# An expert's steps in a new traced order, with three engines' orders pinned to it

## The chip, the cores and the metric

One core of one Trainium2 chip runs the whole program. The metric is device time in microseconds (us); for the kernel before it is 1950.55 us, the median of three runs (1948.15 to 1952.71). The engines are named as in the profile: PE is TensorE (PEld its weight loads), DVE is VectorE, ACT is ScalarE, POOL is GpSimd, SP issues the DMAs.

## What is computed

Two encoder layers on 256 tokens of width 1024, in f32. Each layer has a token mixer, a cross-attention, and a channel mixer, each followed by a residual sum and a layer norm. The channel mixer of the second layer is a mixture of eight experts, of which each token uses two. The change touches that part alone:

```python
D_MODEL, SEQ, N_EXPERTS, TOP_K, D_FF_EXPERT = 1024, 256, 8, 2, 3584

def moe_swiglu(x, w_router, w_gate, w_up, w_down):
    logits = x @ w_router                               # (256, 8)
    top_logit, top_e = lax.top_k(logits, TOP_K)
    top_w = jax.nn.softmax(top_logit, axis=-1)
    # for each expert e and the tokens xs that chose it:
    #   hdn = jax.nn.silu(xs @ w_gate[e]) * (xs @ w_up[e])
    #   y[tokens] += top_w * (hdn @ w_down[e])
```

The weights of one expert are three matrices of 1024 x 3584 f32, 44 MB; all eight are read, whatever the routing gives.

## The kernel before

**Tiling.** `moe` (line 1285) routes the tokens and then calls `expert_run(range(NE), slot, late=True)`. For each expert `gather` collects up to 128 of its tokens with selection matmuls and transposes (`ps_gr`, `ps_gt`) into `xg`, as a high part, a low part and, as `gw`, whole f32. The hidden width 3584 is cut into `NC` = 7 chunks of 512 columns. A chunk has six weight pieces of 1 MiB each: two of `moe_wg` (g0, g1), two of `moe_wu` (u0, u1) and two of `moe_wd` (d0, d1). The products of a chunk are the gate g, the up product u (each 8 contraction slices into one PSUM bank `ps_gu`) and the down product d, which adds four slices into the two banks `ps_ye` and is done one chunk later than g and u.

**Pieces.** `wload` (line 302) issues a piece's DMA into a raw buffer `wr` (SP, line 309) and splits it into `wh`, a copy in fp32r on ScalarE (line 325, two instructions of 128x1024), and `wl = wr - wh` on VectorE (line 331, two instructions). There are nine raw buffers in this part and four pairs of `wh`, `wl`, both used in rotation, so a piece takes over the split pair of the piece four places before it and the raw buffer of the piece nine places before it.

**Two forms of a product.** `products` (line 1389) holds both under a condition on the expert's count of tokens. Over 64 tokens, `passes` makes three matmuls for each slice (`h wh`, `h wl`, `l wh`; lines 1394 to 1396) from the split pieces. Up to 64, `paired` makes one f32 matmul for each slice straight from the raw piece (line 1402), in two halves of the array that `fold` adds up (line 1419, from a copy `fe`, line 1418). The splits stand under the same condition on ScalarE and VectorE and are skipped for an expert with up to 64 tokens. The first form is called dense below and the second sparse.

**Between g, u and d.** `hidden` (line 1440) makes `hs = silu(g) * u`: a Silu on ScalarE (line 1442) and a product on VectorE (line 1443). There is one `hs` buffer. `down` (line 1446) transposes `hs` on TensorE (four instructions into `ps_hT`, line 1449), copies it on ScalarE as `hw` (line 1453) and `hh` (line 423), subtracts for `hl` on VectorE (line 423) and then runs the products with d0 and d1. After an expert's last chunk `combine` scales `ye` and adds it to `x` (lines 1475 to 1501).

**Order.** The program is traced, and a planner then puts each engine's instructions into a fixed queue order by priorities and its own estimate of times. The traced order of a chunk n is: load and split g0, g1; g; copy `fe`; load and split u0, u1; u; copy `fe`; transposes of chunk n-1; `hw`, `hh`, `hl`; load and split d0; product; load and split d1; product; Silu and `hs` of chunk n. The planner is free to deviate, but for one chain: `in_turn` (line 295) pins the split copies of ScalarE, and these alone, in the order in which they are traced. It does this with dependencies that cost no semaphore. What stands under a condition is planned as one block.

Of the kernel before, what the change touches and what calls it, by code (L numbers as in the profile page):

```python
# [10 lines left out]
F32 = mybir.dt.float32  # L11
# [8 lines left out]
P = 128  # L20
# [143 lines left out]
def tile_encoder(ctx: ExitStack, tc: tile.TileContext, a: dict, out: bass.AP, cw: dict):  # L164
# [125 lines left out]

    where = _offsets()

    split = []
# [991 lines left out]
    def moe(l, i, xh, xl, xth, xtl):  # L1285
        with weights("r3", NX, ring=raws), tc.tile_pool(name="mo", bufs=1, reuse_waits="tile") as O:
# [97 lines left out]
            def expert_run(experts, sl, late=False):  # L1384

                NC = FE // 512
                pend = []

                def products(many, ws, h, l, hw, fold=None):


                    def passes():
                        for out, k, wh, wl, _, b, z in ws:
                            T.matmul(out, h[:, k], wh, start=b, stop=False)  # L1394
                            T.matmul(out, h[:, k], wl, start=False, stop=False)  # L1395
                            T.matmul(out, l[:, k], wh, start=False, stop=z)  # L1396

# [23 lines left out]
                parted = lambda many: () if many is None else many[1:]  # L1421

                def gate_up(e, gs, many, c, late=False):
                    pgu, fo = [], None
                    for ws in ("moe_wg", "moe_wu"):
                        pt = abank("ps_gu")
                        todo = []
                        for kh in range(2):
                            wh, wl, w = wload(ws, i * NE + e, kh * 4, 4, c * 512, 512,
                                              [ln_end[0], pd_end[0]] if late else (), parted(many))  # L1430
                            for k4 in range(4):
                                k = kh * 4 + k4
                                todo.append((pt, k, wh[:, k4], wl[:, k4], w[:, k4], k == 0, k == KT - 1))
                        products(many, todo, *gs, fo)
                        pgu.append(pt)
                        if many is not None:
                            fo = folds(e, pt)
                    return pgu, fo

                def hidden(pgu):  # L1440
                    hs = O.tile([P, 512], F32, name="hs", tag="hs", bufs=HSB)
                    A.activation(hs, pgu[0], AF.Silu)
                    V.tensor_mul(hs, hs, pgu[1])  # L1443
                    return hs

                def down(e, many, c, hs, ye, fo):
# [10 lines left out]
                    for f0 in (0, 2):  # L1457

                        ahead = ends if e == experts[-1] and c == NC - 1 and f0 else ()
                        dh, dl, w = wload("moe_wd", i * NE + e, 4 * c + f0, 2, 0, D, ahead, parted(many))  # L1460
                        todo = []
                        for n in range(2):
                            for f in range(2):
                                b, z = c == 0 and f0 + f == 0, c == NC - 1 and f0 + f == 3
                                ns = slice(n * 512, n * 512 + 512)
                                todo.append((ye[n], f0 + f, dh[:, f, ns], dl[:, f, ns], w[:, f, ns], b, z))
                        products(many, todo, hh, hl, hw, fo if f0 else None)

                def combine(e, many, ye, first):

# [29 lines left out]
                            else:  # L1500
                                V.tensor_add(xs, xs, po)

                def flush(fo=None):
                    e, many, c, hs, ye = pend.pop()
                    if c == 0:
                        ye[:] = [bank(psb, "pb", "ps_ye") for _ in range(2)]
                    down(e, many, c, hs, ye, fo)
                    if c == NC - 1:
                        combine(e, many, ye, late and e == experts[0])

                fold = {}
# [6 lines left out]
                for n, e in enumerate(experts):  # L1518
                    gs, many = nxt
                    if many is not None:  # L1520
                        folding(e)
                    ye = []
                    for c in range(NC):
                        pgu, fo = gate_up(e, gs, many, c, late and n + c == 0)
                        if pend:
                            flush(fo if c else None)
                        if fo and not c:
                            fo()
                        hs = hidden(pgu)
                        pend.append((e, many, c, hs, ye))  # L1530
                        if c == NC - 3 and n + 1 < len(experts):
                            nxt = gather(experts[n + 1], sl)
                flush()

            expert_run(range(NE), slot, late=True)
            lp = act.tile([P, 2, D], F32, name="lp", tag="opTh")
# [107 lines left out]
```

## Time and profile before

| what | us |
|---|---|
| median of three runs | 1950.55 |
| the profiled execution: its own time | 1953.46 |
| the profiled execution: span from first to last instruction | 1951.7 |
| first expert's stretch in that span (dense) | 942 to 1104 |
| five sparse experts | 1104 to 1629 |
| two dense experts and the end | 1629 to 1952 |

The page of the profile gives busy time by engine (PE 1733.4 us, DVE 1070.0, ACT 902.8), the span in forty slices with TensorE's granted clock, and the DMA rate in each slice. Busy PE is modelled and grows when the clock is halved, so what tells of lost time in a stretch is the start of one product to the start of the next, and the idle time that stands in brackets in a timeline. In a timeline a row is a run of like instructions: start, length, engine, line, operation, tiles written and read, count, and in brackets the idle time of the engine before it and what ended it.

### The profile page before, as it was taken

What the parts mean: (1) busy time and instruction counts of PE and PEld (TensorE: products, weight loads), DVE (VectorE), ACT (ScalarE), POOL (GpSimd) and SP (SyncE); (2) the same over time, 40 slices, a digit from 0 to 9 for tenths busy, and PEclk for the clock granted to TensorE, in tenths of its full rate; (3) what the DMA queues carried; (4) which work ended last, traced back from release to release, by engine and by line L of the source; (5) the groups of instructions that cost most, each with busy time, mean ns of one, the idle gap of its engine ahead of it and who ended that gap; (6) DMA issues with size and microseconds to landing.
All of it is one profiled execution on the core that took longest, in us unless ns stands there. A gap on an engine that the chain in (4) does not pass through costs nothing. (4 is left out here: it accounts for less than half of the span.)

```text
span 1951.7 us, 29900 instructions
## 1 busy us (share of the span) xinstructions
PE 1733.4 (89%) x11084; PEld 1216.1 (62%) x11084; DVE 1070.0 (55%) x1755; ACT 902.8 (46%) x1651; POOL 257.5 (13%) x248
## 2 busy tenths in 40 slices
PE   6888999999978898998678999899999998999995
PEld 5767779899967776696456633333333334776773
DVE  6887666755568966674565612111111114776785
ACT  4754435555536554452565522122212223776673
POOL 4545310000046453011000000000000000000000
PEclk8988999999989888998788999999999998999997
DMA  6321255455423312551366899999999999878790
GB/s 218 110 102 67 88 194 196 174 177 188 143 81 118 104 67 88 207 224 65 132 256 259 308 405 420 420 419 420 419 420 420 420 420 384 309 282 306 289 359 34
DMA packets 71301, 473.93 MB, mean 243 GB/s; under 512 B 8768, under 2 KB 12224, under 8 KB 15936
## 3 DMA queue, kind: packets, MB, share of 16 engines
q1 hardware_dynamic: 70384, 466.09, 61.7%
q10 hardware_dynamic: 720, 5.24, 0.7%
q8 instruction: 119, 1.95, 0.4%
q14 instruction: 78, 0.64, 0.1%
HBM read 470.26 MB, written 1.05 MB: 241 GB/s over the span
## 5 line engine op out<-in xcount | busy, mean ns | idle before, releaser
L331 DVE TENSOR_TENSOR wl<-wr,wh 128x1024 fp32r<-128x1024 f32 (+4 forms) x530 | 482.5, 965 | 132.9 <-ACT wh L325 131.5
L325 ACT ACTIVATE wh<-wr 128x1024 fp32r<-128x1024 f32 (+1 forms) x564 | 436.0, 845 | 104.4 <-issue 27.9
L1402 PE MATMUL ps_gu<-wr,gw 128*64 128x512 f32 x1120 | 273.7, 615 | 24.6 <-DMA wr<-in_moe_wg_dram 22.6
L1402 PEld LDWEIGHTS ps_gu<-wr,gw 128*64 128x64 f32 x1120 | 81.0, 140 | 178.4 <-issue 141.3
L1453 ACT ACTIVATE hw<-ps_hT 128x512 f32<-128x512 f32 x56 | 33.4, 596 | 334.1 <-PE ps_hT L1449 333.9
L1394 PE MATMUL ps_gu<-wh,xg 128*128 128x512 f32 x336 | 142.6, 424 | 13.6 <-ACT wh L325 13.2
L1402 PE MATMUL ps_ye<-wr,hw 128*64 128x512 f32 x560 | 151.1, 598 | 3.3 <-DMA wr<-in_moe_wd_dram 3.2
L1395 PE MATMUL ps_gu<-wl,xg 128*128 128x512 f32 x336 | 141.2, 420 | 10.3 <-DVE wl L331 10.3
L334 POOL TENSOR_TENSOR wl<-wr,wh 128x384 fp32r<-128x384 f32 (+6 forms) x68 | 103.9, 1549 | 290.3 <-ACT wh L325 289.9
L423 DVE TENSOR_TENSOR hl<-ps_hT,hh 128x512 fp32r<-128x512 f32 x56 | 38.7, 690 | 186.3 <-ACTq L317 107.7
L1396 PE MATMUL ps_gu<-wh,xg 128*128 128x512 f32 x336 | 138.9, 413 | 0.0
L1568 POOL TENSOR_TENSOR x<-x,lp 128x512 f32<-128x512 f32 x1 | 1.8, 1800 | 1021.5 <-ACT x L1567 1021.5
L1443 DVE TENSOR_TENSOR hs<-hs,ps_gu 128x512 f32<-128x512 f32 x56 | 38.3, 685 | 177.8 <-PE ps_gu L1419 173.0
L1418 ACT ACTIVATE fe<-ps_gu 128x512 f32<-128x512 f32 x112 | 66.8, 597 | 102.5 <-PE ps_gu L1419 93.0
L1272 PE MATMUL ps_gu<-xTl,wh 128*128 128x256 f32 x352 | 99.2, 282 | 0.0
L1273 PE MATMUL ps_gu<-xTh,wl 128*128 128x256 f32 x352 | 99.1, 282 | 0.0
L1271 PE MATMUL ps_gu<-xTh,wh 128*128 128x256 f32 x352 | 99.0, 282 | 0.0
L1402 PEld LDWEIGHTS ps_ye<-wr,hw 128*64 128x64 f32 x560 | 49.3, 136 | 79.3 <-issue 56.1
L1394 PEld LDWEIGHTS ps_gu<-wh,xg 128*128 128x128 f32 x336 | 68.3, 203 | 33.2 <-ACT wh L325 16.4
L1395 PEld LDWEIGHTS ps_gu<-wl,xg 128*128 128x128 f32 x336 | 68.4, 203 | 31.4 <-DVE wl L331 17.1
L1419 PE MATMUL ps_gu<-fe,fold 128*64 128x512 f32 x146 | 76.4, 605 | 8.0 <-ACT fe L1418 8.0
L1396 PEld LDWEIGHTS ps_gu<-wh,xg 128*128 128x128 f32 x336 | 67.9, 202 | 15.3
(469 smaller groups left out, 3723.1 us busy)
## 6 DMA issues: line engine op xcount, KB each, us to landing
wr<-in_moe_wg_dram SPq DMA_DIRECT2D x112, 1024.0 KB, 15.8
wr<-in_moe_wu_dram SPq DMA_DIRECT2D x112, 1024.0 KB, 16.3
wr<-in_moe_wd_dram SPq DMA_DIRECT2D x112, 1024.0 KB, 16.1
wr<-in_w_in_dram SPq DMA_DIRECT2D x16, 1024.0 KB, 4.8
wr<-in_ffn_wg_dram SPq DMA_DIRECT2D x11, 1024.0 KB, 4.9
wr<-in_ffn_wu_dram SPq DMA_DIRECT2D x11, 1024.0 KB, 4.9
wr<-in_ffn_wd_dram SPq DMA_DIRECT2D x11, 1024.0 KB, 4.9
wr<-in_xk_dram SPq DMA_DIRECT2D x8, 1024.0 KB, 4.9
```

What stands on the lines that cost most here:

```text
L325: act_i = A.activation(h[:, s], raw[:, s], AF.Copy)
L331: V.tensor_sub(l[:, m], raw[:, m], R_(h[:, m]))
L334: G.tensor_sub(l[:, m], raw[:, m], R_(h[:, m]))
L1271: T.matmul(ps[:, g], wh[:, k, fs], xh[:, k, :], start=k == 0, stop=False)
L1272: T.matmul(ps[:, g], wh[:, k, fs], xl[:, k, :], start=False, stop=False)
L1273: T.matmul(ps[:, g], wl[:, k, fs], xh[:, k, :], start=False, stop=k == KT - 1)
L1394: T.matmul(out, h[:, k], wh, start=b, stop=False)
L1395: T.matmul(out, h[:, k], wl, start=False, stop=False)
L1396: T.matmul(out, l[:, k], wh, start=False, stop=z)
L1402: T.matmul(out[f * HALF:f * HALF + HALF], hw[:, k, :HALF], w, start=ws[j][5], stop=ws[j + 1][6], skip_group_check=True)
L1418: A.activation(fe, pt, AF.Copy)
L1419: return lambda: T.matmul(pt[:HALF], fold[e], fe, start=False, stop=True, skip_group_check=True)
```

## The change

Only `expert_run`, `wload` and `in_turn` change. `in_turn` keeps one chain per engine. Into ScalarE's chain go the split copies, the `fe` copies, `hw`, `hh` and the Silu; into VectorE's the split subtractions, `hl` and the product `hs`; into TensorE's the first matmul of each dense product and the transposes. The last piece's wait for the last `hh` and `hl` (`ahead`) is taken out.

The splits are no longer traced where their product is traced. `order` lists the pieces in the order of before, and `split(n)` loads and splits the next n of them. For a chunk n the traced order becomes: g; split d0 of chunk n-1; transposes of n-1 with `hw`, `hh`, `hl`; split d1 of n-1; `fe` of g; u; split g0 of n+1; `fe` of u; d of n-1 (and `combine` after an expert's last); Silu of n; split g1 and u0 of n+1; product `hs` of n; split u1 of n+1; and `gather` of the next expert after the fifth chunk. The number of instructions of each kind, the DMAs and the buffers stay the same.

```diff
     def in_turn(i):
-        if split:
-            tc.add_manual_dep(i.ins, split[-1].ins.name, mybir.DependencyInfo(
+        e = i.ins.engine
+        if e in pinned:
+            tc.add_manual_dep(i.ins, pinned[e].ins.name, mybir.DependencyInfo(
                 mybir.DependencyClass.NoSync, mybir.DependencyReason.DATA), reason="in_turn")
-        split[:] = [i]
+        pinned[e] = i
...
-                    V.tensor_sub(l[:, m], raw[:, m], R_(h[:, m]))
+                    dve_i = V.tensor_sub(l[:, m], raw[:, m], R_(h[:, m]))
+                    if whole:
+                        in_turn(dve_i)
...
+                turn = lambda many, *ins: [in_turn(i) for i in ins if many is not None]
...
-                        for out, k, wh, wl, _, b, z in ws:
-                            T.matmul(out, h[:, k], wh, start=b, stop=False)
+                        for j, (out, k, wh, wl, _, b, z) in enumerate(ws):
+                            i = T.matmul(out, h[:, k], wh, start=b, stop=False)
+                            if j == 0:
+                                turn(many, i)
...
-                    A.activation(fe, pt, AF.Copy)
+                    in_turn(A.activation(fe, pt, AF.Copy))
...
-                    for f in range(4):
-                        T.transpose(pT[:, f], hs[:, f * P:f * P + P], ident)
+                    turn(many, *[T.transpose(pT[:, f], hs[:, f * P:f * P + P], ident) for f in range(4)])
...
-                        A.activation(hw, pT, AF.Copy)
+                        turn(many, A.activation(hw, pT, AF.Copy))
...
-                    ends = evac_split(hh, hl, pT)
...
+                    turn(many, *evac_split(hh, hl, pT))
...
+                steps = [(e, c) for e in experts for c in range(NC)]
+                order, made = [], {}
+                for n, step in enumerate(steps):
+                    order += [(*step, "g", 0), (*step, "g", 1), (*step, "u", 0), (*step, "u", 1)]
+                    if n:
+                        order += [(*steps[n - 1], "d", 0), (*steps[n - 1], "d", 1)]
+                order += [(*steps[-1], "d", 0), (*steps[-1], "d", 1)]
...
+                def downs(many, e, c, hs, ye, fo):
+                    split()
+                    parts = turned(many, hs)
+                    split()
+                    yield
...
+                    for j in range(2):
+                        down(many, c, 2 * j, parts, ye, made.pop((e, c, "d", j)), fo() if j else None)
+                    if c == NC - 1:
+                        combine(e, many, ye, late and e == experts[0])
+                    yield
...
+                split(4)
+                prev = None
+                for n, (e, c) in enumerate(steps):
...
+                    gates(gs, ptg, ws[0], many, None)
+                    if last:
+                        next(last)
+                    fg = folds(e, ptg) if many is not None else None
+                    gates(gs, ptu, ws[1], many, fg)
+                    split()
+                    if many is not None:
+                        fo[0] = folds(e, ptu)
+                    if last:
+                        next(last)
...
+                    turn(many, A.activation(hs, ptg, AF.Silu))
+                    split(2)
+                    turn(many, V.tensor_mul(hs, hs, ptu))
+                    split()
+                    prev = many, e, c, hs, ye
...
+                run(downs(*prev, lambda: None))
```

## Rows read from the trace of the kernel before

**Rows 1.** Windows: stretch, busy us (count) by engine, clock, DMA share, GB/s.

```profile
942.00:1104.00 162.00, 131.17 (x522) 102.99 (x522) 93.43 (x87) 92.17 (x114) 0.00 (x0) 0.89 0.65 242
...
1104.00:1629.00 525.00, 495.29 (x2120) 183.71 (x2118) 85.33 (x144) 124.87 (x230) 0.00 (x0) 0.98 1.01 418
...
1629.00:1655.00 26.00, 23.17 (x86) 14.85 (x87) 17.66 (x20) 14.76 (x21) 0.00 (x0) 0.87 0.97 384
1655.00:1918.00 263.00, 243.08 (x1021) 190.40 (x1021) 202.72 (x198) 184.00 (x229) 0.00 (x0) 0.96 0.76 292
```

**Rows 2.** Source view, lines 1394 and 1402: count, ns, first and last start.

```profile
L1394 PE MATMUL ps_gu<-wh,xg x336: 387/394/796, 942.3 to 1910.5; 128*128 128x512 f32 x168
...
L1402 PE MATMUL ps_gu<-wr,gw x1120: 592/592/1114, 1104.2 to 1622.1; 128*64 128x512 f32 x187
```

**Rows 3.** Timeline of TensorE, one chunk of expert 6 (columns told above).

```profile
...
1694.26 0.39 PE L1394 MATMUL ps_gu<-wh,xg 128*128 128x512 f32 x1
...
1699.74 0.60 PE L1449 MATMUL ps_hT<-consts,hs 128*128 128x128 f32 x4
1700.09 0.48 PE L1394 MATMUL ps_gu<-wh,xg 128*128 128x512 f32 x1
...
1706.43 0.40 PE L1394 MATMUL ps_ye<-wh,hh 128*128 128x512 f32 x1
...
1711.97 0.40 PE L1394 MATMUL ps_gu<-wh,xg 128*128 128x512 f32 x1
...
```

**Rows 4.** Timeline of ScalarE, the same chunk; idle before in brackets.

```profile
...
1690.81 5.81 ACT L325 ACTIVATE wh<-wr 128x1024 fp32r<-128x1024 f32 x6
1700.43 0.60 ACT L1453 ACTIVATE hw<-ps_hT 128x512 f32<-128x512 f32 x1 [3.82 <-PE ps_hT L1449]
1701.40 2.01 ACT L325 ACTIVATE wh<-wr 128x1024 fp32r<-128x1024 f32 x2
...
```

**Rows 5.** Timeline of VectorE, the chunk before that one.

```profile
...
1684.78 11.77 DVE L331 TENSOR_TENSOR wl<-wr,wh 128x1024 fp32r<-128x1024 f32 x10 [0.25 <-ACT wh L325]
1696.46 0.68 DVE L1443 TENSOR_TENSOR hs<-hs,ps_gu 128x512 f32<-128x512 f32 x1
...
```

**Rows 6.** Timeline of TensorE, expert 0, the third transposes.

```profile
...
1020.45 1.12 PE L1449 MATMUL ps_hT<-consts,hs 128*128 128x128 f32 x4 [6.46 <-DVE hs L1443]
...
```

**Rows 7.** Timeline of ScalarE, the same place.

```profile
...
1008.21 0.59 ACT L1442 ACTIVATE hs<-ps_gu 128x512 f32<-128x512 f32 x1
1014.08 5.79 ACT L325 ACTIVATE wh<-wr 128x1024 fp32r<-128x1024 f32 x6 [5.28 <-issue]
...
```

**Rows 8.** Timeline of VectorE, the same place.

```profile
...
1015.17 4.63 DVE L331 TENSOR_TENSOR wl<-wr,wh 128x1024 fp32r<-128x1024 f32 x4 [5.89 <-ACT wh L325]
1019.72 0.68 DVE L1443 TENSOR_TENSOR hs<-hs,ps_gu 128x512 f32<-128x512 f32 x1
...
```

**Rows 9.** Timeline of TensorE, expert 6, a chunk with a gap.

```profile
...
1763.52 0.60 PE L1449 MATMUL ps_hT<-consts,hs 128*128 128x128 f32 x4
1766.29 0.50 PE L1394 MATMUL ps_gu<-wh,xg 128*128 128x512 f32 x1 [2.18 <-ACT wh L325]
```

**Rows 10.** Timeline of ScalarE, the same place.

```profile
...
1764.21 0.60 ACT L1453 ACTIVATE hw<-ps_hT 128x512 f32<-128x512 f32 x1 [6.55 <-PE ps_hT L1449]
...
1765.18 3.89 ACT L325 ACTIVATE wh<-wr 128x1024 fp32r<-128x1024 f32 x4
...
```

**Rows 11.** Timeline of TensorE, gather work of the next expert inside expert 6.

```profile
...
1717.85 0.71 PE L1372 MATMUL ps_gr<-xtokh,pd 128*128 128x512 f32 x2
...
```

**Rows 12.** Timeline of TensorE, the last chunk and its end.

```profile
...
1917.72 0.66 PE L1449 MATMUL ps_hT<-consts,hs 128*128 128x128 f32 x4 [0.85 <-DVE hs L1443]
1918.22 0.51 PE L1480 MATMUL ps_pT<-gate,pg 128*128 128x1 f32 x4
...
1923.56 0.80 PE L1396 MATMUL ps_ye<-wh,hl 128*128 128x512 f32 x1 [3.21 <-DVE hl L423]
...
1930.25 0.39 PE L1396 MATMUL ps_ye<-wh,hl 128*128 128x512 f32 x1
...
```

More of the change, by code (lines that the diff above doesn't have):

```diff
@@ L1417, in folds, with gates, turned @@
                     fe = O.tile([P, 512], F32, name="fe", tag="fe", bufs=2)
-                    A.activation(fe, pt, AF.Copy)
+                    in_turn(A.activation(fe, pt, AF.Copy))
                     return lambda: T.matmul(pt[:HALF], fold[e], fe, start=False, stop=True, skip_group_check=True)
[L1421 to L1446, printed above, removed]
+                def gates(gs, pt, ws, many, fo):
+                    todo = []
+                    for kh in range(2):
+                        wh, wl, w = ws[kh]
+                        for k4 in range(4):
+                            k = kh * 4 + k4
+                            todo.append((pt, k, wh[:, k4], wl[:, k4], w[:, k4], k == 0, k == KT - 1))
+                    products(many, todo, *gs, fo)
+                def turned(many, hs):
                     pT = bank(psb, "pb", "ps_hT").rearrange("p (f t) -> p f t", f=4)
-                    for f in range(4):
-                        T.transpose(pT[:, f], hs[:, f * P:f * P + P], ident)
+                    turn(many, *[T.transpose(pT[:, f], hs[:, f * P:f * P + P], ident) for f in range(4)])
                     hw = None
@@ L1452, in down @@
                         hw = O.tile([P, 4, P], F32, name="hw", bufs=1)
-                        A.activation(hw, pT, AF.Copy)
+                        turn(many, A.activation(hw, pT, AF.Copy))
                     hh = O.tile([P, 4, P], F32R, name="hh", tag="hh", bufs=2)
                     hl = O.tile([P, 4, P], F32R, name="hl", tag="hl", bufs=2)
-                    ends = evac_split(hh, hl, pT)
[L1457 to L1467, printed above, removed]
+                    turn(many, *evac_split(hh, hl, pT))
+                    return hh, hl, hw
+                def down(many, c, f0, hs, ye, ws, fo):
+                    dh, dl, w = ws
+                    todo = []
+                    for n in range(2):
+                        for f in range(2):
+                            b, z = c == 0 and f0 + f == 0, c == NC - 1 and f0 + f == 3
+                            ns = slice(n * 512, n * 512 + 512)
+                            todo.append((ye[n], f0 + f, dh[:, f, ns], dl[:, f, ns], w[:, f, ns], b, z))
+                    products(many, todo, *hs, fo)
                 def combine(e, many, ye, first):
@@ L1501, in combine @@
                                 V.tensor_add(xs, xs, po)
[L1503 to L1511, printed above, removed]
+                fold, counts = {}, {}
                 def folding(e):
@@ L1533, in expert_run, with split @@
-                flush()
+                steps = [(e, c) for e in experts for c in range(NC)]
[5 more added lines that the diff above has]
+                order += [(*steps[-1], "d", 0), (*steps[-1], "d", 1)]
+                def split(n=1):
+                    for _ in range(n):
+                        if not order:
+                            return
+                        e, c, w, j = key = order.pop(0)
+                        cond = () if counts[e] is None else counts[e][1:]
+                        held = [ln_end[0], pd_end[0]] if late and (e, c) == steps[0] else ()
+                        if w == "d":
+                            made[key] = wload("moe_wd", i * NE + e, 4 * c + 2 * j, 2, 0, D, (), cond)
+                        else:
+                            made[key] = wload("moe_w" + w, i * NE + e, j * 4, 4, c * 512, 512, held, cond)
@@ new lines, in expert_run @@
+                nxt = gather(experts[0], sl)
+                counts[experts[0]] = nxt[1]
+                split(4)
+                prev = None
+                for n, (e, c) in enumerate(steps):
+                    if c == 0:
+                        gs, many = nxt
+                        if many is not None:
+                            folding(e)
+                        ye = []
+                    ptg, ptu = abank("ps_gu"), abank("ps_gu")
+                    ws = [[made.pop((e, c, w, j)) for j in range(2)] for w in "gu"]
+                    fo = [None]
+                    last = downs(*prev, lambda: fo[0] if c else None) if prev else None
+                    gates(gs, ptg, ws[0], many, None)
[4 more added lines that the diff above has]
+                    split()
+                    if many is not None:
+                        fo[0] = folds(e, ptu)
+                    if last:
+                        next(last)
+                    if fo[0] and c == 0:
+                        fo[0]()
+                    hs = O.tile([P, 512], F32, name="hs", tag="hs", bufs=HSB)
+                    turn(many, A.activation(hs, ptg, AF.Silu))
[3 more added lines that the diff above has]
+                    prev = many, e, c, hs, ye
+                    if c == NC - 3 and e != experts[-1]:
+                        nxt = gather(experts[experts.index(e) + 1], sl)
+                        counts[experts[experts.index(e) + 1]] = nxt[1]
```

18 lines of the change are left out of this document (3 added, 15 removed).

## The prediction

> **What bounds the kernel now.** First the windows view, cut where the kind of expert changes [rows 1]; which experts those are is read from the counts [rows 2]. 336 matmuls of line 1394 at 16 for each chunk make 21 dense chunks, three experts; 1120 of line 1402 at 32 make 35 sparse chunks, five experts, that begin at 1104.2. So the first expert is dense (942 to 1104), five are sparse (1104 to 1629), the last two are dense (1629 to 1918). The sparse stretch moves 418 GB/s with a DMA share of 1.01: 35 chunks of 6.29 MB are 220 MB, and 220 MB in 525 us is that same rate. No order of instructions makes it shorter. The dense stretches move 242 and 292 GB/s, so there transfers don't bind, and the clock column (0.89 and 0.96) says that TensorE stood still at times. They are 162 + 26 + 263 us, and all of the change's effect must come from them and from the end.
>
> Then TensorE's timeline of a dense chunk without a long gap [rows 3]: g takes 5.48 us (1694.26 to 1699.74), the transposes 0.35, u 6.34, d 5.54; together 17.71. u has the same 24 matmuls as g, so 0.86 of it is a stall. Without it a chunk is 5.48 + 0.35 + 5.48 + 5.54 = 16.85 us. 21 of these are 354, and the three dense stretches take 451. Last the queues of the other two engines at the places where TensorE stands still, which gives two patterns.
>
> *Expert 0.* The transposes start after 6.46 us of idle time, released by `hs` [rows 6]. Silu was done at 1008.8 [rows 7]; yet `hs` runs at 1019.72, behind subtractions that themselves stood 5.89 us waiting for copies [rows 8], and those copies stood 5.28 us and started at 1014.08, when the previous d was over and gave back its split buffers [rows 7]. So `hs` is queued behind pieces that aren't needed yet and have no buffer. The transposes then take 1.12 us where they take 0.60 elsewhere [rows 3, 6]: the clock is at its lower level, 1.2 GHz, after the idle time.
>
> *Experts 6 and 7.* ScalarE stands 3.82 us in the good chunk and 6.55 in a bad one at `hw`, which needs the transposes, with copies queued behind it [rows 4, 10]. In the bad one TensorE then waits 2.18 us for the first of those copies, at the start of u [rows 9]; in the good one the stall falls into u and is 0.86. So there u's pieces are behind `hw`, although u's pieces need nothing from it.
>
> **The change part by part.** *TensorE's order* in experts 6 and 7 is already g, transposes, u, d; the pins repeat it. Only expert 0 changes, and by as many instructions as before: cost nothing by itself.
>
> *ScalarE and VectorE, a dense chunk.* I walk the new order with TensorE at 16.85 us, g starting at 0, transposes at 5.5, u from 5.8 to 11.3, d from 11.3 to 16.85, a piece's buffers free when its product is done. A piece costs ScalarE 1.9 us (5.81 for six halves [rows 4]) and VectorE 2.35 (11.77 for ten [rows 5]), so a chunk is 11.6 plus five passes of about 0.5 on ScalarE (`hw`, `hh`, two `fe`, Silu), and 14.1 plus two of about 0.65 on VectorE: 14.1 and 15.4 of 16.85. ScalarE: d0 of n-1 5.6 to 7.5 (takes g0's pair); `hw`, `hh` to 8.5; d1 to 10.4; `fe`; g0 of n+1 11.4 to 13.3; `fe`, Silu to 14.3; g1 to 16.2; u0 to 18.1; u1 to 20.0. VectorE follows each copy: u0 to 20.1, `hs` to 20.8, u1 to 23.2. The transposes of n want `hs` at 16.85 + 5.5 = 22.35: slack 1.6 us. u wants u0 at 22.7 and the second half u1 at 25.4: slack 2.2. d0 and d1 come 2 us or more ahead. If a buffer comes free in the middle of its product instead, all slacks grow by about 2. The pinned waits that stand in front of others (d0's copy ahead of `hw`, u0's subtraction ahead of `hs`) thus cost nothing, covered by g and d; if that cover failed, the cost is the second rival's. Both patterns above go: `hs` is behind u0 only, u's copies are ahead of `hw`.
>
> *DMA queue.* Pieces are loaded in the same order by the same queue. A chunk in 16.85 us needs 6.29 MB, 373 GB/s, under the 418 that the sparse stretch holds [rows 1].
>
> *The sum for the stretches.* Expert 0: g and u once without a d, 11.0; six chunks of 16.85, 101.1; the next expert's gather on TensorE, two selections of 1.0 (to the next row [rows 3, 11]: four matmuls) and two transposes of 0.35, 2.7. That is 115. To it I add frictions that rows bound but don't fix: 5 us for the first chunk, where ScalarE and VectorE have no lead (below: 0; above: the 6.46 gap), and 6 for the gather's five ScalarE and VectorE passes that push the splits beyond the slack (0 to 12, two gaps of the kind of rows 6). 126 against 162: 36 saved. The first chunk of expert 6 shares its 26 us with the last sparse d and a combine; its data arrive at the DMA's pace (0.97), so I take 6 off (0 to 9). The other 13 chunks: 13 x 16.85 = 219, one gather 2.7, one combine (eight matmuls at 0.23 and 0.8 of small ones) 2.6, and 6 each for their unpinned passes: 236 against 263, 27 saved (39 without friction, 0 if gaps stay). *The end:* from the last transposes at 1917.72 to the last down matmul at 1930.6 are 12.9 us, with 3.21 idle at `hl`, which waits behind a subtraction of the last pieces [rows 12]. New, those pieces are split before the last `hs`: 0.7 + 1.2 of hand-over + 5.54 + 1.4 for `hl` is 8.8: 4 saved.
>
> Together 36 + 6 + 27 + 4 = 73. The profiled execution took 1953.46 (span 1951.7), so 1880 for its like; the median is 2.9 lower: **1877.5**. With all frictions at nothing it is 47 + 9 + 39 + 4 = 99, 1851.5. The frictions are thus 26 us; doubled, they leave 47 of gain, 1903.5. Both ends are kept.
>
> *Sparse stretch.* The splits are skipped there, but ScalarE and VectorE must still pass each condition, and a raw buffer is given back only then. In the new order each piece's condition is passed before TensorE's own product with it (d1's after `hl`, which is after g), so I take 0; above, a delay of 0.3 us in each of 35 chunks would be 10.
>
> *Buffers.* The copies of expert 0 did stand 5.28 us for a split buffer [rows 7], and the change adds none. What speaks against buffers as the whole cause is that Silu was done 11 us before `hs` ran [rows 7, 8]: `hs` itself needed no buffer. The Trainium skill ("Perfetto Trace Analysis", Optimization Strategy) has a rule against this change: the same gap repeating on the engine that should be saturated can mean that there is too little memory for the next tile. By it the gaps of expert 0 would move and not go, and the time would be that of the first rival; the trace agrees with it as far as the 5.28 us go.
>
> **The rivals.** *Four split pairs are the limit.* The gap in expert 0 moves from `hs` to the next split, since the buffers still come free at the same products; only u's stalls and the end are won: 27 + 4, 1919. For: the 5.28 us at 1014.08. Against: the walk, in which every buffer is free before its copy's turn or is not needed within 2 us. Chance 0.14 (1905 to 1945).
>
> *Slower: `hs` behind u0 closes a loop.* u0's pair is d0's of the chunk before. Where VectorE comes late by more than the slack of 1.6 us, `hs` comes after the end of g, the transposes wait, the clock falls to the lower level, d is late, and so is the buffer of the next u0. It decides at 1.6 us; gather and combine put more than that on VectorE. If it doesn't recover, all 21 chunks take what expert 0's take now, 162 us for 6.6 chunks or 24.5 each: expert 0 stays, the 13 chunks become 319 instead of 263, 1950 + 56 = 2006; decaying after each gather, some 1970. For: expert 0 shows that very loop today. Against: VectorE has 1.4 us spare in every chunk, and d0 is freed at the middle of d. Chance 0.11.
>
> *It doesn't do what it says*, or what is won is given back: the unpinned gather and combine are placed so that the chains wait for them, or transfers run out. Against: the dense stretches would ask for 373 of 418 GB/s, and VectorE for 15.4 of 16.85 us. 1947 to 1954. Chance 0.04.
>
> **How the numbers follow.** Forecast 0.71 (1850 to 1905), buffers 0.14, loop 0.11, nothing 0.04. The range 1850 to 1925 holds the first and the nearer half of the second: 0.8. A measurement of this kernel tells 0.2%, 4 us, from no change: faster 0.85, same 0.04, slower 0.11.
>
> **What would show it.** In expert 0 order g, transposes, u, d, with no idle before the transposes and a stretch near 126 us; in experts 6 and 7 `hw` preceded by copies, not by 4 to 6 us of idle time, chunks near 16.9; the sparse stretch at 525 and 418 GB/s; granted clock of the dense stretches near 1. I am wrong if the transposes still wait for `hs`, if the sparse stretch grows, or if a gather's chunk costs over 10 us more than its neighbours.

## The result and the profile after

The changed kernel takes 1885.22 us, the median of four runs (1883.41 to 1888.69), against 1951.63 for the kernel before beside it: a ratio of 0.9665, 95% interval 0.9645 to 0.9684. The profiled execution took 1884.93 us (span 1883.0), 68.5 less than the one of before.

The windows view, cut at the same events as [rows 1] (first product of expert 0, first sparse product, first product of expert 6, second one there, last transposes); columns as there:

```profile
939.50:1063.00 123.50, 119.03 (x522) 95.25 (x522) 92.38 (x87) 91.84 (x114) 0.00 (x0) 0.99 0.83 319
1063.00:1593.90 530.90, 492.76 (x2119) 187.01 (x2118) 89.08 (x147) 129.23 (x233) 0.00 (x0) 0.98 1.01 416
1593.90:1616.90 23.00, 19.89 (x84) 13.58 (x84) 13.02 (x17) 12.51 (x19) 0.00 (x0) 0.93 0.90 349
1616.90:1853.30 236.40, 230.11 (x1024) 184.74 (x1022) 206.38 (x201) 188.69 (x231) 0.00 (x0) 1.00 0.85 326
```

Expert 0 takes 123.5 us where it took 162.0, the 13 later chunks 236.4 where they took 263. The granted clock of the dense stretches is 0.99 and 1.00 (0.89 and 0.96 before). The sparse stretch is 5.9 us longer.

Three timelines of one clean chunk of expert 0. TensorE first, the start of each product (to be held against [rows 3] and [rows 6]):

```profile
972.78 0.40 PE L1399 MATMUL ps_gu<-wh,xg 128*128 128x512 f32 x1
...
978.29 0.60 PE L1439 MATMUL ps_hT<-consts,hs 128*128 128x128 f32 x4
978.65 0.47 PE L1399 MATMUL ps_gu<-wh,xg 128*128 128x512 f32 x1
...
984.22 0.40 PE L1399 MATMUL ps_ye<-wh,hh 128*128 128x512 f32 x1
...
989.73 0.40 PE L1399 MATMUL ps_gu<-wh,xg 128*128 128x512 f32 x1
```

No bracket, no idle time: g 5.51, transposes 0.36, u 5.57, d 5.51, together 16.95 us. Then ScalarE (against [rows 4], [rows 7]):

```profile
975.80 2.01 ACT L326 ACTIVATE wh<-wr 128x1024 fp32r<-128x1024 f32 x2 [0.76 <-ACT wh L326]
978.99 0.60 ACT L1443 ACTIVATE hw<-ps_hT 128x512 f32<-128x512 f32 x1 [1.18 <-PE ps_hT L1439]
979.48 0.59 ACT L426 ACTIVATE hh<-ps_hT 128x512 fp32r<-128x512 f32 x1
979.96 2.01 ACT L326 ACTIVATE wh<-wr 128x1024 fp32r<-128x1024 f32 x2
```

`hw` still waits for the transposes, but 1.18 us instead of 3.82 to 6.55, and what stands behind it is only d1, which TensorE wants 8 us later; u's pieces and d0 have gone ahead. Last VectorE (against [rows 5], [rows 8]):

```profile
970.86 4.62 DVE L332 TENSOR_TENSOR wl<-wr,wh 128x1024 fp32r<-128x1024 f32 x4
975.40 0.68 DVE L1563 TENSOR_TENSOR hs<-hs,ps_gu 128x512 f32<-128x512 f32 x1
976.00 4.62 DVE L332 TENSOR_TENSOR wl<-wr,wh 128x1024 fp32r<-128x1024 f32 x4
980.54 0.68 DVE L426 TENSOR_TENSOR hl<-ps_hT,hh 128x512 fp32r<-128x512 f32 x1
```

`hs` runs two pieces ahead of `hl` and is done at 976.08, 2.2 us before the transposes; in the next chunk it is 3.5 us.

### The profile page after: what moved, and what is told of

It is laid out like the page before. It is cut to its first block, busy times and chain, and to the rows that moved or that the text cites. A ratio compares the mean times of both kernels' runs of the same rounds, so it can differ in the third digit from the quotient of the medians.

```text
span 1883.0 us, 29952 instructions
## 1 busy us (share of the span) xinstructions
PE 1700.3 (90%) x11084; PEld 1204.5 (64%) x11084; DVE 1067.5 (57%) x1755; ACT 907.7 (48%) x1651; POOL 257.0 (14%) x248
## 5 line engine op out<-in xcount | busy, mean ns | idle before, releaser
L1409 PE MATMUL ps_gu<-wr,gw 128*64 128x512 f32 x1120 | 274.8, 610 | 16.6 <-DMA wr<-in_moe_wg_dram 16.5
L1409 PEld LDWEIGHTS ps_gu<-wr,gw 128*64 128x64 f32 x1120 | 85.0, 139 | 164.7 <-issue 158.0
L1399 PE MATMUL ps_gu<-wh,xg 128*128 128x512 f32 x336 | 135.1, 402 | 1.2 <-ACT wh L326 0.8
L1402 PE MATMUL ps_gu<-wl,xg 128*128 128x512 f32 x336 | 132.2, 393 | 1.5 <-DVE wl L332 1.5
L1403 PE MATMUL ps_gu<-wh,xg 128*128 128x512 f32 x336 | 132.5, 394 | 0.0
L1399 PEld LDWEIGHTS ps_gu<-wh,xg 128*128 128x128 f32 x336 | 63.8, 190 | 16.4 <-ACT wh L326 2.9
L1402 PEld LDWEIGHTS ps_gu<-wl,xg 128*128 128x128 f32 x336 | 63.9, 190 | 15.6 <-DVE wl L332 2.3
L1403 PEld LDWEIGHTS ps_gu<-wh,xg 128*128 128x128 f32 x336 | 63.7, 190 | 14.5
```

The lines of the kernel that those rows point to most:

```text
L1399: i = T.matmul(out, h[:, k], wh, start=b, stop=False)
L1409: T.matmul(out[f * HALF:f * HALF + HALF], hw[:, k, :HALF], w, start=ws[j][5], stop=ws[j + 1][6], skip_group_check=True)
```

## The experiments

Each variant is read by the same events. All times in us; "to the last T" is from expert 6's first product to the last transposes. The start of expert 0 in the profiled executions lies anywhere from 935.3 to 944.9, in a part that no edit is aimed at (only those of the buffers reach into it), so that the whole time can't settle differences of a few us. The stretches can, though each is read from one profiled execution.

| kernel | whole time (ratio to before, 95%) | expert 0 | sparse | to the last T | after it |
|---|---|---|---|---|---|
| before | 1951.6 | 162.0 | 525.0 | 288.5 | 33.9 |
| changed | 1885.2 (0.9645 to 0.9684) | 123.5 | 530.9 | 259.3 | 29.8 |
| order_only | 1951.6 (0.9985 to 1.0015) | 162.5 | 525.0 | 287.0 | 29.7 |
| no_pe | 1976.2 (1.0116 to 1.0149) | 140.2 | 539.1 | 324.4 | 31.1 |
| no_dve | 1909.9 (0.9779 to 0.9812) | 139.6 | 530.7 | 269.1 | 29.5 |
| no_act | 1912.6 (0.9789 to 0.9822) | 127.1 | 526.0 | 285.5 | 31.1 |
| b_pins | 2106.6 (1.0779 to 1.0834) | 201.2 | 528.4 | 406.8 | 32.6 |
| late_hs | 1900.3 (0.9718 to 0.9765) | 130.8 | 530.6 | 270.7 | 29.8 |
| hs_early | 1929.9 (0.9870 to 0.9911) | 139.0 | 529.0 | 288.2 | 33.9 |
| pairs5 | 1883.3 (0.9635 to 0.9687) | 124.5 | 535.2 | 254.3 | 31.1 |
| b_pairs5 | 1926.7 (0.9844 to 0.9896) | 139.0 | 529.6 | 281.1 | 34.5 |
| fe_first | 1885.4 (0.9638 to 0.9682) | 125.9 | 527.2 | 260.0 | 29.5 |
| g0_late | 1890.7 (0.9665 to 0.9710) | 129.5 | 527.5 | 260.8 | 29.7 |
| fe_mixed | 1886.3 (0.9645 to 0.9671) | 123.5 | 526.4 | 260.0 | 29.6 |

### The new traced order without the new pins: order_only

```diff
                             if j == 0:
-                                turn(many, i)
+                                pass
...
-                    in_turn(A.activation(fe, pt, AF.Copy))
+                    A.activation(fe, pt, AF.Copy)
...
```

All pins of the change are taken out but those on the split copies, which the kernel before had.

> The new traced order alone: of the pins only those on ScalarE's split copies are left, which the kernel before had too. Theory (the fixed queue order carries the gain): the planner lays out the three queues as it did before, so 1950 us, within 5 of the kernel before, and expert 0 again near 162 us with an idle time of some 6 us before its transposes. Rival (the traced order carries it, the pins only repeat it): 1885, expert 0 at 123.

Measured: 1951.6, and every stretch up to the last transposes within 1.5 us of before. From expert 0 on, the queues of TensorE, ScalarE and VectorE are, by the tiles that their instructions write and read, those of the kernel before, but for two fold matmuls and the last pieces: the planner undoes the traced order. Without the pins nothing is left of the dense stretches' gain. Only the end is an exception. There the last pieces are split ahead of the last `hs` without the new pins too, and it takes 29.7 us, as in the changed kernel, where before took 33.9. These 4.2 us come from the traced order or from the wait `ahead` that was taken out; the two weren't separated, and the whole time doesn't show them.

### One engine's pins taken away: no_pe, no_dve, no_act

The same edit for one engine each (for VectorE the subtractions, `hs` and `hl`; for ScalarE `fe`, `hw`, `hh`, Silu, its split copies staying pinned).

> The changed kernel with no pins on TensorE. The planner then puts half of the down product of one chunk behind g of the next and ahead of the transposes. Theory: that half holds its split pair through g, and u's second piece, which takes that pair, comes 1 to 4 us late in each of the 21 dense chunks: 1905 to 1965, most likely 1930. Rival (only the order of ScalarE and VectorE matters, TensorE's is free): 1885 within 5.

Measured: 1976.2, slower than before and outside my range. The direction was the theory's, the mechanism not: u's pieces come only 0.5 us late. TensorE's idle times in expert 6:

```profile
1677.91 0.66 PE L1439 MATMUL ps_hT<-consts,hs 128*128 128x128 f32 x4 [0.85 <-DVE hs L1563]
...
1682.07 0.63 PE L1399 MATMUL ps_ye<-wh,hh 128*128 128x512 f32 x1 [3.50 <-ACT hh L426]
1683.53 0.79 PE L1403 MATMUL ps_ye<-wh,hl 128*128 128x512 f32 x1 [0.40 <-DVE hl L426]
...
1695.99 0.50 PE L1402 MATMUL ps_gu<-wl,xg 128*128 128x512 f32 x1 [0.50 <-DVE wl L332]
...
1702.42 0.66 PE L1439 MATMUL ps_hT<-consts,hs 128*128 128x128 f32 x4 [0.85 <-DVE hs L1563]
```

The transposes now stand right behind d and the next d right behind the transposes. Both hand-overs (0.85 for `hs`, 3.50 and 0.40 for `hh` and `hl`) lie open, where the pinned order puts g ahead of the one and u behind the other. This chunk takes 24.5 us, the stretch 324.4. Seven of the stretch's 14 chunks show the second wait too; without it a clean chunk takes 18.2 us.

> The changed kernel with no pins on VectorE. The planner then puts hs one piece later, behind the subtraction of u1 too. In the trace of the changed kernel hs ends 2.2 to 3.5 us before the transposes in clean chunks, and one piece is 2.35 us. Theory (slack decides, a small overrun costs only itself): nothing in most chunks, 1 to 2 us where a gather or a combine lies: 1885 to 1897, most likely 1889. Rival (a late hs closes a loop through the split pairs): expert 0 back at 150 to 162 us and 1915 or more.

Measured: 1909.9, between the two. The planner put `hs` not one piece later but two, behind u1 and d0, and `hl` behind d1, from expert 0's second chunk on. VectorE there:

```profile
983.97 2.36 DVE L332 TENSOR_TENSOR wl<-wr,wh 128x1024 fp32r<-128x1024 f32 x2 [2.88 <-ACT wh L326]
986.24 0.68 DVE L424 TENSOR_TENSOR hl<-ps_hT,hh 128x512 fp32r<-128x512 f32 x1
...
999.02 0.68 DVE L1561 TENSOR_TENSOR hs<-hs,ps_gu 128x512 f32<-128x512 f32 x1
```

with the transposes of TensorE at 981.14 and 999.76:

```profile
999.76 0.66 PE L1437 MATMUL ps_hT<-consts,hs 128*128 128x128 f32 x4 [1.48 <-DVE hs L1561]
```

That is a closed loop, and its length can be read off: 2.83 us from the transposes to the first subtraction (it waits for a copy queued behind `hw` and `hh`), 2.27 and 0.60 to the end of `hl`, 12.18 for five pieces, 0.74 from `hs` to the next transposes: 18.62, the chunk's time. The loop of the prediction's slower rival exists; it costs 1.7 us a chunk and 5.6 at the gather, not 7.6.

> The changed kernel with pins on ScalarE's split copies alone, not on its fe, hw, hh and Silu. The planner then sets fe of g ahead of u1's copy in expert 0, and Silu ahead of more copies later; hw stays behind u's copies. Theory: u1 has over 2 us to spare, so little is lost: 1883 to 1893, most likely 1887; at the border from the sparse to the dense experts the first piece no longer stands ahead of fe, which can give 3 back. Rival (the pins on ScalarE are what removed u's stalls): the 27 us of the other 13 chunks return, 1910 or more.

Measured: 1912.6. It came out as the rival said: the stretch of experts 6 and 7 loses 26.2 of the 29.1 us that it had won. I had read the queue wrongly; u1 and d0 do fall behind `hw` here:

```profile
1646.26 0.60 ACT L1443 ACTIVATE hw<-ps_hT 128x512 f32<-128x512 f32 x1 [4.89 <-PE ps_hT L1439]
1646.75 0.59 ACT L426 ACTIVATE hh<-ps_hT 128x512 fp32r<-128x512 f32 x1
1647.23 0.60 ACT L1425 ACTIVATE fe<-ps_gu 128x512 f32<-128x512 f32 x1
1647.71 5.80 ACT L326 ACTIVATE wh<-wr 128x1024 fp32r<-128x1024 f32 x6
```

4.89 us of idle time ahead of `hw`, then three passes and three pieces in a row: the pattern of [rows 4, 10], and chunks of 18.7 to 19.2. The sparse stretch, at 526.0, is 4.9 shorter than with these pins, which the last experiments take up.

So the three engines' pins answer for different places: TensorE's for every chunk, VectorE's for expert 0 and what follows a gather or combine, ScalarE's for experts 6 and 7.

### The old order, pinned: b_pins

The kernel before with the same pins in its own traced order.

> The kernel before in its own traced order (g, u, transposes, d0, d1, then Silu and hs), with the same pins on all three engines. Theory (what is pinned matters, not that it is pinned): d0's copy then starts only behind hw, so each down product waits some 3.5 us for its first piece and each chunk takes about 20.5 us: 1935 to 1990, most likely 1957; expert 0 near 145. Rival (a fixed order of any kind does it): within 10 of 1885.

Measured: 2106.6, 8% slower than before and far beyond the range. ScalarE in expert 0:

```profile
1023.79 0.60 ACT L1425 ACTIVATE fe<-ps_gu 128x512 f32<-128x512 f32 x1 [9.97 <-PE ps_gu L1403]
1024.28 3.88 ACT L326 ACTIVATE wh<-wr 128x1024 fp32r<-128x1024 f32 x4
1033.87 0.60 ACT L1425 ACTIVATE fe<-ps_gu 128x512 f32<-128x512 f32 x1 [5.71 <-PE ps_gu L1403]
```

Each product's `fe` stands ahead of the next product's copies, so copies and products alternate: 9.97 and 5.71 us of idle ScalarE, TensorE waiting for the first copy of each product in turn, most dense chunks 28 to 32 us, at a granted clock of 0.84 in expert 0. My expectation had counted d's wait alone. A pin is worth what its order is worth: the same pins gain 3.4% or lose 8%.

### How far `hs` may move: late_hs, hs_early

```diff
-                    turn(many, V.tensor_mul(hs, hs, ptu))
                     split()
+                    turn(many, V.tensor_mul(hs, hs, ptu))
```

> The changed kernel, hs pinned behind the subtraction of u1 of the next chunk instead of ahead of it: exactly one piece (2.35 us) later, still ahead of d0's. Theory (hs only must not stand behind a piece whose pair is given back by the product that the transposes wait behind): u1 takes the pair of d1 of the chunk before, free 5.5 us before the transposes, so no loop closes; the slack of 2.2 to 3.5 us swallows the 2.35 in clean chunks, and a gather or combine costs up to 2: 1885 to 1897, most likely 1889, expert 0 within 4 of 123.5. Rival (slack alone decides, and what is lost comes back each chunk): like the kernel without pins on VectorE, expert 0 near 140 and 1905 or more.

Measured: 1900.3, above the theory's range and short of the rival's. Clean chunks keep 16.9 to 17.0, so no loop closes at one piece. But where a gather or combine takes the slack, 2.35 us of delay cost more than the 2 I allowed: 3.28 us of idle time and a slower start behind it.

```profile
1034.16 2.36 DVE L332 TENSOR_TENSOR wl<-wr,wh 128x1024 fp32r<-128x1024 f32 x2 [2.10 <-ACT wh L326]
1036.44 0.68 DVE L1564 TENSOR_TENSOR hs<-hs,ps_gu 128x512 f32<-128x512 f32 x1
```

```profile
1037.18 0.96 PE L1439 MATMUL ps_hT<-consts,hs 128*128 128x128 f32 x4 [3.28 <-DVE hs L1564]
```

The gather's chunk takes 24.9 us instead of 21.5, and expert 0 130.8.

The other way, `fe` of u, Silu and `hs` ahead of all four pieces of the next chunk:

```diff
-                    split()
                     if many is not None:
                         fo[0] = folds(e, ptu)
...
-                    split(2)
                     turn(many, V.tensor_mul(hs, hs, ptu))
-                    split()
+                    split(4)
```

> The changed kernel with fe of u, Silu and hs ahead of all four pieces of the next chunk (g0, g1, u0, u1), instead of behind g0 and u0. Theory: the border gives 3.4 us as with fe first; hs is ready 8 us ahead of the transposes, so the idle times of 0.85 and 0.40 us before transposes in expert 0 go too; g0's copy starts 1.7 us later, and hs no longer stands behind it: 1878 to 1883, most likely 1880. Rival (hs and Silu at the head of their queues hold the pieces back until u is done, and d0, behind four pieces, comes late): each dense chunk takes 17.5 us or more, 1895 or more.

Measured: 1929.9, and chunks of 18.9 to 19.0: the rival's sign, for another reason. `hs` can't run early at all. VectorE in expert 6 (Silu is over at 1647.33; the matmul behind d's last starts at 1651.48):

```profile
1643.77 2.35 DVE L332 TENSOR_TENSOR wl<-wr,wh 128x1024 fp32r<-128x1024 f32 x2
1651.75 0.69 DVE L1561 TENSOR_TENSOR hs<-hs,ps_gu 128x512 f32<-128x512 f32 x1 [5.62 <-PE ps_ye L1403]
1652.35 11.44 DVE L332 TENSOR_TENSOR wl<-wr,wh 128x1024 fp32r<-128x1024 f32 x10
```

It is released by the down product. The reason stands in the code: the sparse form folds u's halves inside the second part of d (`down(..., fo() if j else None)`), both forms stand under one condition, and `hs` reads u after that block; so a dense expert waits for the block too. (This cause is read from row and code; no run took it away. The same releaser stands at the last `hs` of the changed kernel, 1852.52, with 1.07 us.) At the head of VectorE's queue `hs` held five pieces back for 5.62 us. Its earliest place is the end of d, its latest the transposes 5.5 us later. Behind u0 lies in between.

### A fifth pair of split buffers: pairs5, b_pairs5

`WL = 3` and `NRAW = 5`: one pair more, two raw buffers fewer, in the changed kernel and in the kernel before.

> The changed kernel with a fifth pair of split buffers, paid for with two of its seven raw buffers. Theory (in the new order every pair is free before its turn): dense stretches within 2 us of 123.5 and 259.3; the sparse stretch can only lose by fewer raw buffers, 0 to 10: 1883 to 1895. Rival (four pairs are still the limit at gathers and combines): the chunks of 21.5 and 24.5 us shrink by 2 or more each, 1878 or less.

> The kernel before with a fifth pair of split buffers, paid for with two of its seven raw buffers. Rival (too few buffers made the gaps): expert 0's idle time before the transposes goes, 162 becomes 130 or less, and the time is 1920 or less. Theory (hs and u's copies stand too far back in their queues): one more piece is split ahead of the release, which is 2.35 of the 6.46 us in expert 0 at best, and u's pieces stay behind hw in experts 6 and 7: expert 0 at 148 to 162, the rest as before, 1935 to 1955.

Nine raw buffers become seven here (`NRAW` counts only some of them), and the memory stays the same: a pair takes the place of two raw buffers.

Measured: in the changed kernel 1883.3, not to be told from it. Expert 0 is the same (124.5), and so is the gather's chunk (21.4). Experts 6 and 7 gain 5.1, against the theory: about 2.1 each in the chunk with expert 5's combine and in that with expert 6's (24.5 becomes 22.4, the rival's sign), the rest mostly in expert 6's first g. The sparse stretch grows by 4.3, which I put down to the two raw buffers.

In the kernel before 1926.7, outside the theory's range and short of the rival's: expert 0 goes from 162.0 to 139.0, more than the 148 I set as its best, while experts 6 and 7 keep most of their u stalls (281.1). But this run changed two things. The planner, which now has five pairs to plan with, also lays out another order. Between an `hl` and the next `hs` in expert 0, VectorE makes 12, 6 and 8 subtractions of half a piece, where the kernel before makes 10, 10 and 8. Behind the six, `hs` waits for no piece but for d:

```profile
995.72 6.90 DVE L331 TENSOR_TENSOR wl<-wr,wh 128x1024 fp32r<-128x1024 f32 x6 [4.12 <-ACT wh L325]
1005.39 0.69 DVE L1443 TENSOR_TENSOR hs<-hs,ps_gu 128x512 f32<-128x512 f32 x1 [2.77 <-PE ps_ye L1396]
```

The prediction weighed a rule of the Trainium skill ("Perfetto Trace Analysis", Optimization Strategy): a repeating gap can mean that there is too little memory for the next tile. The trace agrees with it for at most 23 of expert 0's 38 us, since the pair and the planner's other order share them, and what each is worth was not tried. The pinned order won all 38, and 29 in experts 6 and 7, with the buffers as they were.

### What grew in the sparse stretch: fe_first, g0_late, fe_mixed

The border from expert 5 to expert 6 in the changed kernel, ScalarE, then TensorE:

```profile
1580.17 0.60 ACT L1425 ACTIVATE fe<-ps_gu 128x512 f32<-128x512 f32 x1
1589.48 2.00 ACT L326 ACTIVATE wh<-wr 128x1024 fp32r<-128x1024 f32 x2 [8.72 <-DMA wr<-in_moe_wg_dram]
1591.39 0.58 ACT L1425 ACTIVATE fe<-ps_gu 128x512 f32<-128x512 f32 x1
```

```profile
1592.02 1.97 PE L1426 MATMUL ps_gu<-fe,fold 128*64 128x512 f32 x2 [5.30 <-ACT fe L1425]
1593.92 0.80 PE L1399 MATMUL ps_gu<-wh,xg 128*128 128x512 f32 x1
...
1601.02 0.60 PE L1439 MATMUL ps_hT<-consts,hs 128*128 128x128 f32 x4
```

Expert 6's g0 is the first piece that is split again. Its copy waits 8.72 us for its transfer at the head of ScalarE's queue, pinned ahead of `fe` of expert 5's last u. TensorE, which only wants that `fe`, stands 5.30 us and does the two fold matmuls in 1.97 us (1.02 in the kernel before). Its g then takes 7.10 us where 5.5 is usual, but it took 8.1 in the kernel before too (1629.25 to 1637.38). In the kernel before copy and `fe` stood the other way round:

```profile
1623.66 0.60 ACT L1418 ACTIVATE fe<-ps_gu 128x512 f32<-128x512 f32 x1 [2.63 <-PE ps_gu L1419]
...
1628.14 4.84 ACT L325 ACTIVATE wh<-wr 128x1024 fp32r<-128x1024 f32 x5 [3.40 <-DMA wr<-in_moe_wg_dram]
```

Three kernels move `fe` of u:

```diff
-                    split()
                     if many is not None:
                         fo[0] = folds(e, ptu)
+                    split()
```

(fe_first; g0_late puts Silu ahead of that split too; fe_mixed keeps the old place in expert 0's first chunk only.)

> The changed kernel with one swap in the traced order: fe of u ahead of the split of the next chunk's g0, not behind it. Theory (at the border from expert 5 to expert 6 the copy of g0 waits at the head of ScalarE's queue for its transfer, with fe of u behind it, and this is what the sparse stretch grew by): first g of expert 6 comes 3.4 us sooner after its piece has landed, the sparse stretch 530.9 becomes 527 to 528. In dense chunks g0's copy, which now runs in the second half of u, starts 1.7 us later, under the slack of 2.2. 1880 to 1885, most likely 1881.5. Rival (the border is paid by the transfers): 530.9 stays, 1885 within 2; or the 1.7 us are felt at gathers and combines as the 2.35 of the late hs were, and 1888 or more.

> The changed kernel with fe of u and Silu ahead of the split of the next chunk's g0; hs stays behind u0. Theory: as fe first at the border (527 to 528 instead of 530.9); ScalarE's two passes ahead of g0 are 0.5 us more than with fe alone, still inside the slack of hs in clean chunks: 1880 to 1888, most likely 1882.5, and slower than the kernel with hs ahead of all four pieces, since only hs stands at its limit. Rival (what comes first on ScalarE doesn't matter outside the border): the same time as with fe first within 1 us.

Measured: 1885.4 and 1890.7, the first at the edge of its range, the second above it. The sparse stretch shrinks by 3.7 and 3.4, as expected. ScalarE, then TensorE with `fe` first:

```profile
1587.67 0.60 ACT L1425 ACTIVATE fe<-ps_gu 128x512 f32<-128x512 f32 x1 [2.62 <-PE ps_gu L1426]
1593.51 2.00 ACT L326 ACTIVATE wh<-wr 128x1024 fp32r<-128x1024 f32 x2 [5.25 <-DMA wr<-in_moe_wg_dram]
```

```profile
1590.84 1.02 PE L1426 MATMUL ps_gu<-fe,fold 128*64 128x512 f32 x2
1594.62 0.50 PE L1399 MATMUL ps_gu<-wh,xg 128*128 128x512 f32 x1 [2.76 <-ACT wh L326]
```

The copy still waits, but `fe` is no longer behind it, and the fold takes 1.02 us. Now it is g that waits 2.76 us for the copy, and it takes 8.1 us again. So the stretch behind gives 0.7 to 1.4 of the gain back (260.0 and 260.8 to the last T). The other dense chunks don't feel the 1.7 us. What I had not expected is expert 0, which loses 2.4 and 6.0 us, nearly all in its first chunk: there the transfer is early, and g0's copy ahead of `fe` is work done in time.

```profile
946.90 2.00 ACT L326 ACTIVATE wh<-wr 128x1024 fp32r<-128x1024 f32 x2
951.91 0.60 ACT L1425 ACTIVATE fe<-ps_gu 128x512 f32<-128x512 f32 x1 [3.02 <-PE ps_gu L1403]
```

is the changed kernel; with `fe` first the two stand at

```profile
953.88 0.60 ACT L1425 ACTIVATE fe<-ps_gu 128x512 f32<-128x512 f32 x1 [4.92 <-PE ps_gu L1403]
954.37 1.99 ACT L326 ACTIVATE wh<-wr 128x1024 fp32r<-128x1024 f32 x2
```

> The changed kernel with fe of u ahead of the split of g0 in all chunks but the very first, which keeps g0's copy in front. Theory (the swap gains 3.7 us at the border because the transfer is late there, and loses 2.4 us in expert 0's first chunk because the transfer is early there; one order for all chunks can't have both): expert 0 back at 123.5, the sparse stretch at 527.2, together 941 us from expert 0's first product to the end, against 943.5 for the changed kernel and 942.7 with fe first: 1880 to 1885, most likely 1882. Rival (the two differences are only chance from run to run): 943 or more for that sum, 1885.

Measured: 123.5 and 526.4, so both places can be had, and 939.5 from expert 0's first product to the end against 943.5 in the changed kernel. The whole time, 1886.3, is above the range and doesn't show it: in the profiled execution the untouched part ahead took 5.4 us more (944.9 against 939.5). A gain of 4 us in the stretches is read, a faster kernel is not shown.

## Why the prediction came out right, and where it was off

The forecast was 1877.5; it is 1885.2. A gain of 73 was predicted, 68.5 measured between the profiled executions. The mechanism was right in the dense stretches, and one term was wrong, the sparse stretch. That the sum is only 4.5 off is in part luck: two terms fell short by 9.6 together, and expert 0 with 2.5 and the start of expert 0 with 2.7 made up for half of it. Term by term:

- **Expert 0**, 126 predicted, 123.5 measured. The clean chunk is 16.95 where 16.85 was worked out. The first chunk's friction is right (transposes 21.8 us after the first product, 16.5 + 5.3), the gather's was 3, not 6.
- **The 13 chunks**, 236 against 236.4. The u stalls are gone as worked out. The friction, 10.8 over chunks of 16.95 where 12 was put, is near in sum but not in its parts: 2.8 at the gather and 5.0 at the combine, where 6 each were put, and 2.0 ahead of the first and 1.0 ahead of the last transposes, where nothing was.
- **The end**: from the last transposes to the last down matmul 7.9 (1853.27 to 1861.2; before 12.9, [rows 12]), predicted 8.8. 5.0 saved; what comes behind them gave 0.9 back. The reason given, that the last pieces are split before the last `hs`, holds, but the pins aren't what does it (order_only).
- **Expert 6's first chunk**, 6 predicted, 2.3 measured (25.3 to 23.0). This term was mis-sized. g is not the reason: it took 7.10 us, 1.0 less than before. The combine is one. It waits for `yl`, which VectorE runs behind a subtraction of a later piece (1613.01 to 1615.37):

```profile
1616.08 0.50 PE L1486 MATMUL ps_co<-yl,pgT 128*128 128x512 f32 x1 [3.06 <-DVE yl L1482]
```

That wait isn't the work of VectorE's pins: in no_dve, without them, it is 3.06 us as well.

- **The sparse stretch**, 0 predicted, 5.9 lost. This is the step that failed, and the growth of this stretch was one of the prediction's own signs of being wrong. I had asked whether a skipped split's condition would be passed in time, and it is: behind its first 41 us the stretch moves 420 GB/s, as before. The loss is at the edges. At the end, where a split is no longer skipped, a pinned copy at the head of a queue waits for a transfer, and the `fe` behind it is wanted at once. With that undone the stretch gives back 3.7 (fe_first), 3.4 (g0_late), 4.5 (fe_mixed) and 4.9 (no_act), so that 1 to 2.5 us stay. They point to transfers at the start of the stretch. Its first 41 us in the changed kernel and before:

```profile
1063.00:1104.00 41.00, 39.17 (x172) 16.74 (x171) 14.14 (x22) 12.61 (x21) 0.00 (x0) 1.00 0.95 373
```

```profile
1104.20:1145.20 41.00, 40.58 (x179) 17.33 (x179) 13.97 (x22) 12.96 (x22) 0.00 (x0) 1.00 1.00 393
```

20 GB/s less over 41 us is, by estimate, 2 us at the 420 GB/s at which both go on. No variant but order_only, whose queues are those of before, brought the stretch back to 525. What slows the first pieces wasn't tried and stays open.

- The rest, 2.7 us, is the start of expert 0, which moves from run to run.

38.5 + 29.1 (experts 6 and 7 to the last transposes) + 4.2 (behind them) + 2.7 - 5.9 = 68.6.

**The reasons.** That `hs` is queued behind pieces without a buffer, and u's pieces behind `hw`, is shown: with `hs` back behind d0 (and `hl` behind d1) 16 us of expert 0 come back (no_dve), and with u1 and d0 back behind `hw` 26 us of experts 6 and 7 (no_act). One argument was weaker than it looked. From Silu's end to `hs` in [rows 7, 8] I counted 11 us of queueing; hs_early shows that `hs` waits for d in any case, and d had only just ended when the copies started at 1014.08. Some 5.6 of the 11 were queueing. That TensorE's pins "cost nothing and repeat the order" missed their use: without them the planner, which now meets other queues, builds an order worse than before's. They are worth 91 us.

**The rivals.** "Four split pairs are the limit" is false for expert 0 in the new order (pairs5: unchanged), true there for some 5 us in experts 6 and 7, and open for the old order, where a fifth pair and another order together took 23 us off expert 0 (b_pairs5). The loop behind `hs` is real, but decides later than at the 1.6 us I gave: at one piece, 2.35, it costs only where a gather or combine has used the slack (late_hs); at two, with `hl` behind d1, it closes (no_dve). The measured slack is 2.2 to 3.5. Buffers come free in the middle of a product, which the prediction had left open: d0's copy, which takes over g0's pair, starts at 975.80, while g runs from 972.78 to 978.29.

## What to carry to other kernels

Where engines run fixed queues, look at a gap not only for what releases it but for what the released instruction stood behind, and give each instruction its earliest and latest time (`hs`: end of d, transposes) before choosing its place. An order needs every engine of the loop: with one left free 25 to 91 us of time came back, where all the pins gain 66, and the same pins on a wrong order lost 155. Then walk the first pass and the borders by themselves, since a wait that is covered in the steady loop stands open where a transfer is late or the neighbour's work is skipped.

## What the runs showed of the chip

- An idle TensorE can pay twice. Behind 5.30 us of idle time the granted clock was 0.50 from 1592 to 1596, the lower of the two levels, and two fold matmuls took 1.97 us instead of 1.02; over the whole window of 23 us the clock was 0.93. Taking that wait away (fe_first) gave the sparse stretch back 3.7 us and not more, since a wait of 2.76 took its place. Idle times of 0.85 before transposes, as at 961.32 in expert 0, left the window at 0.99.
- As far as row and code tell, a condition makes one unit of what stands under it, for the waits too: in hs_early a VectorE instruction stood 5.62 us until a block of matmuls was over of which only the branch not taken writes what it reads.
